# Who gets the eight PSUM banks in a two-layer hybrid decoder trunk: two for turned tiles, three for the input projection, the output projection in the scores' banks

## The chip, the cores and the metric

The kernel runs on one core of a Trainium2 chip. The metric is device time in microseconds (us) of the whole launch: inputs are in HBM at its start, the output is in HBM at its end. The work is done by TensorE (matrix multiplications and, through a multiplication with the identity, transposes), VectorE (DVE), ScalarE (ACT), GpSimd (POOL, here only a few memsets) and the DMA queues. Matmul results land in PSUM, which has eight banks; a bank holds one tile of 128 x 512 fp32 values. "Turned" below means transposed on TensorE.

## The reference

The sequence has S = 512 tokens of width D = 1024, the trunk has two layers, everything is fp32. Cut to what matters:

```python
for l in range(2):
    h = rms_norm(x, norm_mix_pre[l])
    q_da, k_da, v_da, q_r, k_r, v_r, g_r, u_pool = split(h @ w_in[l])     # 1024 -> 2560
    o_da   = diff_attention(q_da, k_da, v_da, ...)   # 4 heads: softmax(q1 k1) - lam * softmax(q2 k2), causal, times v
    o_ret  = retention(q_r, k_r, v_r, g_r, ...)      # 4 heads, chunks of 128: inside a chunk, and a state carried on
    o_pool = pool_mixer(u_pool, ...)                 # means over trailing windows 2/4/8/16, then 64x64 products
    mix = concat([o_da, o_ret, o_pool]) @ w_out[l]   # 1024 -> 1024
    x = x + rms_norm(mix, norm_mix_post[l])
    h = rms_norm(x, norm_mlp_pre[l])
    gate, val = split(causal_conv3(h @ w_up[l]))     # 1024 -> 5632
    x = x + rms_norm((gelu(gate) * val) @ w_down[l], norm_mlp_post[l])    # 2816 -> 1024
```

## The kernel before

**Tiles.** The tokens make four tiles of 128 (t or i, 0 to 3). Weights stay in no buffer for long: they stream through in units of 512 KB, read by SP's DMA queue into three raw buffers. ACT rounds each unit to the short format that TensorE multiplies fast (`wa`/`wb`, the high part, L275/L286), DVE takes what rounding left over (the low part, L276/L287). A product of full accuracy is three matmuls: high x high, high x low, low x high. The same holds for activations: `ht` is the normed input turned, high and low part; `qh`/`ql` the queries, `ks` the keys, `mixc` the concatenated head outputs.

**Order.** TensorE's order is written out: `mm` and `tr` (L321 to L325; all rows of the trace for TensorE carry L322 for a matmul and L325 for a transpose) chain each instruction to the one before. The main line of a layer is the input projection in five groups of 512 columns (`in_item`, group s = 0 queries, 1 keys, 2 values, 3 retention's keys and values, 4 gate and pooled input), the output projection, the up projection in 11 groups (`up_item`) and the down projection (`project` is both the output and the down projection). Between its matmuls stand small steps of the head groups, as tasks, each with a due time in the table PLACE; `serve` lets a task issue its next step when TensorE's count of columns has reached that time and what it names as needed has been issued. The order of ACT and DVE is set by a scheduler that sees which instruction waits for which.

**The tasks,** each of which opens a PSUM tile:
- `turned` in `qk_done` (L601): a query or key tile, scaled by ACT (L598), is turned into a `b` tile; `q_split` (ACT L616, DVE L619) or `k_split` (ACT L625, DVE L626) reads it out in two parts.
- `unit_a` (L676): scores of one head, map and token tile into an `s` tile; DVE masks, ACT takes the exponential (L689).
- `unit_b` (L698): the softmax weights turned into a `b` tile, which ACT copies out (L705).
- `unit_c` (L708): weights times values into the `o` tile.
- `unit_e` (L737): a token tile's head outputs turned into a `b` tile, read out by ACT (L734) and DVE (L735).
- `row_line` (L648), `ret_1` to `ret_4` (L749 to L812), `pool_mm` (L831): further users of `b`. `ret_3` also opens the update of the state, `bu`, in an `s` tile, which DVE reads at L785.
- Of the input projection's `m` tiles, ACT reads queries and keys at L598 and values at L629, DVE the retention values at L637 to L639, and the last group at L664 and, for the pooled input, L669. `finish_token` (L437) reads the tiles of the output and down projections.

**Banks.** `bank(tag)` takes a tile from a pool that deals by turns among the banks of its tag:

```python
BUFS = {"m": 4, "s": 2, "b": 1, "o": 1}
def bank(tag, shape=(P, 512)):
    return pp.tile(list(shape), F32, tag=tag, name=nm("ps_" + tag), bufs=BUFS[tag])
```

So the projections have four banks, the scores two, everything turned one, the values one. The first matmul into a tile waits until all readers of the tile that stood in its bank before are done. The output projection takes two banks for each token tile: `m`, `m` for tiles 0 and 1, `s`, `s` for 2, and `b`, `o` for 3.

Of the kernel before, what the change touches and what calls it, by code (L numbers as in the profile page):

```python
# [11 lines left out]
F32 = mybir.dt.float32  # L12
# [8 lines left out]
P = 128  # L21
# [4 lines left out]
KC = D // P  # L26
DFF = 2816
NFF = DFF // P
# [109 lines left out]
def tile_trunk(ctx: ExitStack, tc: tile.TileContext, x, xt, win, wout, wup, wdown, gpost, par, lam, const, out):  # L138
# [14 lines left out]
    def nm(s):  # L153
        uid[0] += 1
        return f"{s}_{uid[0]}"

    BUFS = {"m": 4, "s": 2, "b": 1, "o": 1}

    def bank(tag, shape=(P, 512)):
        return pp.tile(list(shape), F32, tag=tag, name=nm("ps_" + tag), bufs=BUFS[tag])  # L160

    ROLES = {"any": list(range(8)), "p0": [0, 1, 2], "p1": [3, 4], "aT": [5, 6], "on": [7], "g": [2]}
    turn = {r: 0 for r in ROLES}
# [383 lines left out]
    q_order = (0, 1, 2, 3)  # L547

    for l in range(DEPTH):
# [222 lines left out]
        def ret_3(c):  # L772
            ind, kq, kz = ret.pop(c)
            b = bank("b")
            if c > 0:
                mm(b[:, 0:256], lhsT=kq[:, P:2 * P], rhs=st_bd[0], start=True, stop=False, skip_group_check=True)
            for h in range(4):
                mm(b[:, 64 * h:64 * h + 64], lhsT=ind[:, h * P:(h + 1) * P], rhs=vr[:, c, 64 * h:64 * h + 64],
                          start=(c == 0), stop=True, skip_group_check=True)
            if c < NT - 1:  # L780
                bu = bank("s")
                mm(bu[:, 0:256], lhsT=kz, rhs=vr[:, c, :], start=True, stop=True)
                ns = one.tile([P, 256], F32, tag="state", name=nm("state"), bufs=2)
                bm = C("bm").unsqueeze(2).to_broadcast([P, 4, 64])
                ve.tensor_tensor(out=ns.rearrange("p (h d) -> p h d", h=4), in0=bu[:, 0:256].rearrange("p (h d) -> p h d", h=4), in1=bm, op=ALU.mult)  # L785
                if c > 0:
                    ve.scalar_tensor_tensor(ns, st_bd[0], C("cd"), ns, op0=ALU.mult, op1=ALU.add)
                st_bd[0] = ns
            oc = rtok[c // 2][:, c % 2, :]
            ov = oc.rearrange("p (h d) -> p h d", h=4)  # L790
            se.copy(oc, b[:, 0:256])
            sq = t2("p1", 256)
            se.activation(sq, oc, AF.Square)
            ss = small(4)
            ve.tensor_reduce(ss, sq.rearrange("p (h d) -> p h d", h=4), axis=AX.X, op=ALU.add)
            r = head_rsqrt(ss, 4, 64)
            ve.tensor_tensor(out=ov, in0=ov, in1=r.unsqueeze(2).to_broadcast([P, 4, 64]), op=ALU.mult)
            on_of[c] = oc
# [95 lines left out]
        banks = {}  # L894

        def in_item(s, j, t, rel, *cs):
            if (s, t) not in banks:
                banks[s, t] = bank("m")
            u = u0 + 4 * s + j
            (item_feat if s == 4 else item_tok)(banks[s, t], j, t, u, *cs)  # L900
            if rel:
                release(u)
            if j == 3:
                with ahead(300):
                    dones[s](banks.pop((s, t)), t)

        for s in range(5):
            od = q_order if s == 0 else range(NT)
            plan = [(j, t) for ts in (od[0:2], od[2:4]) for j in range(4) for t in ts]
            if s == 0 and l:  # L910
                plan = [(j, t) for t in od for j in range(4)]
            elif s == 0:
                plan = [(0, t, (c,)) for c in range(2) for t in od] + [(1, t) for t in od] + [(j, t) for t in od for j in (2, 3)]
            for n, (j, t, *cs) in enumerate(plan):
                if t not in row and j == 2:
                    row_factors(t)
                main(lambda: in_item(s, j, t, all(x[0] != j for x in plan[n + 1:]), *cs), u0 + 4 * s + j,
                     *[(l, "xT", x) for x in ((t,) if s < 4 else range(NT))])
            if s == 1:
                for gen in (turns(), values(), outputs(), scores()):  # L920
                    task(gen)
            if s == 3:
                for c in range(NT):
                    task(retention(c))
# [3 lines left out]
        def project(kn, lhs, plan, tags, u0, gain, needs, then, hook=None):  # L928
            ys = {}
            gp = None  # L930

            def item(k, t, cols, rel):
                if t not in ys:
                    ys[t] = [bank(tg) for tg in tags[t]]
                lh, ll = lhs(k, t)
                wh, wl = halves[u0 + k]
                for a, w, first in ((lh, wh, True), (lh, wl, False), (ll, wh, False)):
                    for h in cols:
                        mm(ys[t][h], lhsT=a, rhs=w[:, h * 512:(h + 1) * 512],
                           start=(k == 0 and first), stop=(k == kn - 1 and w is wh and a is ll))  # L940
                    serve(512 * len(cols))
                if rel:
                    release(u0 + k)

            for n, (k, t, *cols) in enumerate(plan):
                if hook is not None:
                    hook(k)
                if k == kn - 1 and gp is None:
                    gp = gain()
                main(lambda: item(k, t, cols or (0, 1), all(x[0] != k for x in plan[n + 1:])), u0 + k, *needs(k, t))  # L950
                if k == kn - 1 and cols != [0]:
                    with ahead(300):
                        finish_token(t, ys[t], gp)
                        then(t, tags[t])
# [29 lines left out]
        def mixed(k, t):  # L984
            if k == 0 and t == 2:
                return (l, "e", NT - 1), (l, "r4", NT - 1), (l, "p", 0), (l, "p", 1)
            return ((l, "e", t) if k < 4 else (l, "r4", t) if k < 6 else (l, "p", k - 6),)
        project(KC, mix_lhs, plan, {0: ("m", "m"), 1: ("m", "m"), 2: ("s", "s"), 3: ("b", "o")},
                unit[0], lambda: load_gain(2 * l), mixed, next_mlp)
        state["space"] = []  # L990
        unit[0] += KC
# [41 lines left out]
        bks = {}  # L1033

        def up_item(g, j, ft, a, b):
            tags = ["m"] * 4 if g % 2 == 0 else ["s", "s", "b", "o"]
            fresh = (g, ft) not in bks
            if fresh:
                bks[g, ft] = bank(tags[ft])
            u = u0 + 4 * g + j  # L1040
            k = dict(skip_group_check=True) if g == 1 and ft < 2 else {}
            item_feat(bks[g, ft], j, ft, u, a, b, fresh or not k, **k)
            if b == S and ft == 3:
                release(u)
            if b == S and j == 3:
                up_done(bks.pop((g, ft)), g, ft)
# [38 lines left out]
        def act_lhs(k, t):  # L1085
# [5 lines left out]
        plan += [(k, t) for k in range(2, NFF - 7) for t in range(NT)]  # L1091
        plan += [(k, t) for t in q_order[:3] for k in range(NFF - 7, NFF)]
        plan += [(k, q_order[3], h) for h in range(2) for k in range(NFF - 7, NFF)]
        project(NFF, act_lhs, plan, {0: ("s", "s"), 1: ("b", "o"), 2: ("m", "m"), 3: ("m", "m")},
                unit[0], lambda: gain2, lambda k, t: (), store if l == DEPTH - 1 else next_mixer, hook)
        state["space"] = []
        unit[0] += NFF
# [42 lines left out]
```

## Time and profile before

| | us |
|---|---|
| runs | 1155.54, 1155.96, 1156.54 |
| median | 1155.96 |
| the profiled execution | 1154.14 |
| its span in the trace | 1152.3 |

The span goes from the first to the last instruction that the profiler shows; the execution's own time has what lies around it as well. Clocks in the trace count from the span's start. In rows of the profile, engines are PE (TensorE's matmuls), PEld (its weight loads), DVE, ACT, POOL and SP; `ps_b<-cst,t` is a tile written from tiles read, with the numbers of tiles left out; an instruction's row gives its start, its duration, how many were grouped (x4), and in brackets the idle time of the engine just ahead of it, with the instruction that ended last among those that it waited for. In the first layer the input projection with the tasks runs to about 160 us, the output projection opens there, and the second layer's mixer begins about 610 us.

### The profile page before, as it was taken

To read this page: it belongs to the slowest core of one execution; us is meant where nothing else is said; L and a number is where in the kernel's file an instruction comes from. 1 tells how busy PE (TensorE), PEld (TensorE's weight loads), DVE (VectorE), ACT (ScalarE), POOL (GpSimd) and SP (SyncE) were. 2 spreads that over 40 slices of the span, in tenths; PEclk is the share of its full clock that TensorE was granted. 3 is DMA by queue.
4 is the path that set the end of the run, shared out by engine and by line. 5 is a ranking of instruction groups with operands and counts; after the bars stand their busy time and mean duration, and the time that the engine had idled before them with its cause. 6 is when DMAs were issued, how large, how long until landed. Compare 5 with 4: busy or idle time off the path is not lost.

```text
span 1152.3 us, 14840 instructions
## 1 busy us (share of the span) xinstructions
PE 1135.6 (99%) x5474; PEld 943.6 (82%) x5474; DVE 740.6 (64%) x1669; ACT 547.5 (48%) x1049; POOL 12.0 (1%) x20
## 2 busy tenths in 40 slices
PE   9999999999999999999999999999999999999997
PEld 6788778988888888888888887789888888888885
DVE  6988696877556457423777896877855655663224
ACT  6966553565444345313466754444744434452211
POOL 1000000000000000000000000000000000000000
PEclk9999999999999999999999999999999999999999
DMA  8411131332222232224033111303323232223311
GB/s 325 147 55 56 55 113 40 111 128 91 100 102 85 101 106 95 98 95 143 4 103 114 59 61 45 111 20 127 121 100 108 78 107 104 98 80 104 105 42 55
DMA packets 31320, 109.22 MB, mean 95 GB/s; under 512 B 3728, under 2 KB 4240, under 8 KB 31248
## 3 DMA queue, kind: packets, MB, share of 16 engines
q1 hardware_dynamic: 29808, 105.11, 26.4%
q10 hardware_dynamic: 1440, 3.17, 0.8%
q8 instruction: 43, 0.70, 0.2%
q14 instruction: 29, 0.24, 0.1%
HBM read 106.16 MB, written 2.10 MB: 94 GB/s over the span
## 4 chain that ended last, share of the span: by engine, by line
PE 93%; DVE 2%; ACT 2%; DMA 1%; issue 0%; SPq 0%; DVEq 0%; ACTq 0%
PE ps_m L322 52%; PE ps_s L322 18%; PE ps_b L322 10%; PE ps_o L322 10%; PE ps_b L325 2%; DMA raw<-in_win 1%; ACT t L689 1%; ACT wa L286 1%; PE ps_m L325 0%; DMA raw<-in_wout 0%; DVE ks L626 0%; DVE wb L287 0%; PE ps_s L325 0%; DVE wa L287 0%; DVE sm L687 0%
## 5 line engine op out<-in xcount | busy, mean ns | idle before, releaser
L322 PE MATMUL ps_m<-ht,wb 128*128 128x512 f32 (+1 forms) x768 | 197.9, 366 | 0.0
L322 PE MATMUL ps_m<-ht,wa 128*128 128x512 f32 (+1 forms) x768 | 197.2, 365 | 0.0
L287 DVE SCALAR_TENSOR_TENSOR wa<-raw,par,wa 128x512 fp32r<-128x512 f32 x128 | 95.7, 748 | 145.8 <-ACT wa L286 145.6
L286 ACT ACTIVATE wa<-raw,par 128x512 fp32r<-128x512 f32 x128 | 92.2, 721 | 188.0 <-PE ps_m L322 93.6
L322 PEld LDWEIGHTS ps_m<-ht,wa 128*128 128x128 f32 x768 | 135.2, 189 | 22.9 <-issue 1.0
L322 PEld LDWEIGHTS ps_m<-ht,wb 128*128 128x128 f32 x768 | 135.2, 189 | 22.7 <-issue 1.0
L322 PE MATMUL ps_m<-wa,ht 128*128 128x512 f32 x512 | 147.9, 396 | 0.4 <-ACT ht L504 0.3
L322 PE MATMUL ps_m<-wb,ht 128*128 128x512 f32 x448 | 129.3, 394 | 0.0
L322 PEld LDWEIGHTS ps_m<-wa,ht 128*128 128x128 f32 x512 | 93.4, 189 | 19.2 <-ACT ht L504 1.0
L276 DVE TENSOR_TENSOR wb<-raw,wa 128x1024 fp32r<-128x1024 f32 x38 | 46.6, 1225 | 81.9 <-ACT wa L275 81.9
L287 DVE SCALAR_TENSOR_TENSOR wb<-raw,par,wb 128x512 fp32r<-128x512 f32 x128 | 95.7, 747 | 4.5 <-ACT wb L286 4.4
L322 PEld LDWEIGHTS ps_m<-wb,ht 128*128 128x128 f32 x448 | 82.5, 188 | 16.3
L286 ACT ACTIVATE wb<-raw,par 128x512 fp32r<-128x512 f32 x128 | 91.9, 719 | 3.9 <-PE ps_m L322 3.2
L275 ACT CAST wa<-raw 128x1024 fp32r<-128x1024 f32 x38 | 39.9, 1051 | 86.7 <-PE ps_m L322 78.7
L322 PE MATMUL ps_s<-ht,wb 128*128 128x512 f32 (+1 forms) x264 | 69.1, 370 | 0.0
L322 PE MATMUL ps_s<-ht,wa 128*128 128x512 f32 (+1 forms) x264 | 69.0, 370 | 0.0
L322 PE MATMUL ps_m<-wa,c 128*128 128x512 f32 x224 | 65.7, 399 | 1.3 <-DVE pooled L669 1.3
L322 PEld LDWEIGHTS ps_s<-ht,wa 128*128 128x128 f32 x264 | 47.5, 188 | 8.6
L322 PEld LDWEIGHTS ps_s<-ht,wb 128*128 128x128 f32 x264 | 47.4, 188 | 8.4
L322 PEld LDWEIGHTS ps_m<-wa,c 128*128 128x128 f32 x224 | 41.6, 188 | 11.4 <-DVE pooled L669 2.2
L689 ACT ACTIVATE t<-ps_s,sm 128x128 f32<-128x128 f32 (+3 forms) x64 | 33.5, 527 | 21.5 <-DVE sm L687 18.8
L1010 ACT ACTIVATE t<-ps_m,par 128x512 f32<-128x512 f32 x48 | 36.5, 774 | 12.0 <-PE ps_m L322 12.0
(314 smaller groups left out, 1884.6 us busy)
## 6 DMA issues: line engine op xcount, KB each, us to landing
raw<-in_wup SPq DMA_DIRECT2D x88, 512.0 KB, 3.4
raw<-in_wdown SPq DMA_DIRECT2D x44, 512.0 KB, 3.4
raw<-in_win SPq DMA_DIRECT2D x39, 512.0 KB, 3.6
raw<-in_wout SPq DMA_DIRECT2D x16, 512.0 KB, 3.5
xs<-in_x SPq DMA_DIRECT2D x4, 512.0 KB, 9.6
gain<-in_gpost ACTq DMA_DIRECT2D x4, 512.0 KB, 5.0
t<-in_xt SPq DMA_DIRECT2D x3, 512.0 KB, 6.1
out<-xs SPq DMA_DIRECT2D x4, 256.0 KB, 2.0
```

Source lines behind the costliest of these rows:

```text
L275: se.copy(h, r)
L276: ve.tensor_tensor(out=lo, in0=r, in1=h.bitcast(F32), op=ALU.subtract)
L286: se.activation(a, x, AF.Copy, scale=sc)
L287: ve.scalar_tensor_tensor(b, x, sc, a.bitcast(F32), op0=ALU.mult, op1=ALU.subtract)
L322: in_order(te.matmul(out, lhsT=lhsT, rhs=rhs, **k))
L325: in_order(te.transpose(out, in_, ident))
L689: se.activation(p[:, 0:n], sb[:, 0:n], AF.Exp, bias=top, accum_out=sums[:, m:m + 1])
L1010: se.activation(acc, ps, AF.Identity, bias=conv[:, f, 3:4], scale=conv[:, f, 2:3])
```

## The change

It replaces the pool's dealing by a table of banks. What is turned (`b`) gets two, numbers 6 and 3, the input projection (`m`) three instead of four, 0 to 2; the scores keep two (4, 5), the values one (7). The output projection, the up and the down projection no longer name roles but banks, written out for each token tile or group (OUT_BANKS, DOWN_BANKS, UP_BANKS). The input projection's first group of four tiles opens in four banks that are named too: 0, 1, 2 and 4 in the first layer, 4, 5, 1 and 2 in the second. The state's update `bu` moves from `s` to `b`. In whole:

```diff
--- before.py
+++ after.py
@@ -154,10 +154,22 @@
         uid[0] += 1
         return f"{s}_{uid[0]}"
 
-    BUFS = {"m": 4, "s": 2, "b": 1, "o": 1}
-
-    def bank(tag, shape=(P, 512)):
-        return pp.tile(list(shape), F32, tag=tag, name=nm("ps_" + tag), bufs=BUFS[tag])
+
+
+    BANKS = {"m": (0, 1, 2), "s": (4, 5), "b": (6, 3), "o": (7,)}
+    took = dict.fromkeys(BANKS, 0)
+
+    def bank(role, shape=(P, 512)):
+        k = role
+        if role in BANKS:
+            k = BANKS[role][took[role] % len(BANKS[role])]
+            took[role] += 1
+        return pp.tile(list(shape), F32, tag=f"bank{k}", name=nm(f"ps_{role}"), bufs=1)
+
+
+    OUT_BANKS = {0: (4, 5), 1: (1, 2), 2: (0, 7), 3: (6, 3)}
+    DOWN_BANKS = {0: (0, 7), 1: (6, 3), 2: (4, 5), 3: (1, 2)}
+    UP_BANKS = ((4, 5, 1, 2), (0, 7, 6, 3))
 
     ROLES = {"any": list(range(8)), "p0": [0, 1, 2], "p1": [3, 4], "aT": [5, 6], "on": [7], "g": [2]}
     turn = {r: 0 for r in ROLES}
@@ -778,7 +790,7 @@
                 mm(b[:, 64 * h:64 * h + 64], lhsT=ind[:, h * P:(h + 1) * P], rhs=vr[:, c, 64 * h:64 * h + 64],
                           start=(c == 0), stop=True, skip_group_check=True)
             if c < NT - 1:
-                bu = bank("s")
+                bu = bank("b")
                 mm(bu[:, 0:256], lhsT=kz, rhs=vr[:, c, :], start=True, stop=True)
                 ns = one.tile([P, 256], F32, tag="state", name=nm("state"), bufs=2)
                 bm = C("bm").unsqueeze(2).to_broadcast([P, 4, 64])
@@ -895,7 +907,7 @@
 
         def in_item(s, j, t, rel, *cs):
             if (s, t) not in banks:
-                banks[s, t] = bank("m")
+                banks[s, t] = bank("m" if s else ((4, 5, 1, 2) if l else (0, 1, 2, 4))[q_order.index(t)])
             u = u0 + 4 * s + j
             (item_feat if s == 4 else item_tok)(banks[s, t], j, t, u, *cs)
             if rel:
@@ -904,6 +916,7 @@
                 with ahead(300):
                     dones[s](banks.pop((s, t)), t)
 
+        took["m"] = 0
         for s in range(5):
             od = q_order if s == 0 else range(NT)
             plan = [(j, t) for ts in (od[0:2], od[2:4]) for j in range(4) for t in ts]
@@ -985,7 +998,7 @@
             if k == 0 and t == 2:
                 return (l, "e", NT - 1), (l, "r4", NT - 1), (l, "p", 0), (l, "p", 1)
             return ((l, "e", t) if k < 4 else (l, "r4", t) if k < 6 else (l, "p", k - 6),)
-        project(KC, mix_lhs, plan, {0: ("m", "m"), 1: ("m", "m"), 2: ("s", "s"), 3: ("b", "o")},
+        project(KC, mix_lhs, plan, OUT_BANKS,
                 unit[0], lambda: load_gain(2 * l), mixed, next_mlp)
         state["space"] = []
         unit[0] += KC
@@ -1033,7 +1046,7 @@
         bks = {}
 
         def up_item(g, j, ft, a, b):
-            tags = ["m"] * 4 if g % 2 == 0 else ["s", "s", "b", "o"]
+            tags = UP_BANKS[g % 2]
             fresh = (g, ft) not in bks
             if fresh:
                 bks[g, ft] = bank(tags[ft])
@@ -1091,7 +1104,7 @@
         plan += [(k, t) for k in range(2, NFF - 7) for t in range(NT)]
         plan += [(k, t) for t in q_order[:3] for k in range(NFF - 7, NFF)]
         plan += [(k, q_order[3], h) for h in range(2) for k in range(NFF - 7, NFF)]
-        project(NFF, act_lhs, plan, {0: ("s", "s"), 1: ("b", "o"), 2: ("m", "m"), 3: ("m", "m")},
+        project(NFF, act_lhs, plan, DOWN_BANKS,
                 unit[0], lambda: gain2, lambda k, t: (), store if l == DEPTH - 1 else next_mixer, hook)
         state["space"] = []
         unit[0] += NFF
```

All line numbers behind the table are 12 higher in the changed kernel (13 from the loop over the input projection's groups on): L322 becomes L334, L325 L337.

No instruction is added or removed; TensorE, SP and POOL issue in the same order as before. What differs is which semaphores TensorE's instructions wait for and, on ACT and DVE, the places of a few instructions. In the order below, a name carries its role and two running numbers, `x3` are three instructions alike, and the brackets name the engines whose semaphores an instruction waits for.

TensorE in the first layer's mixer, where the weights of one head (`t2_270`) and of the next (`t2_290`) are turned, with input projection between and scores (`ps_s`) behind; in the trace of before the second turning is at 123.25. Before:

```order
L322 MATMUL ps_m_282_1305<-wa_198_970,ht_82 128x512 x3
L325 MATMUL ps_b_314_1449<-cst_80,t2_270_1256 128x128 [waits DVE_49]
L325 MATMUL ps_b_314_1449<-cst_80,t2_270_1256 128x128 x3
L322 MATMUL ps_m_282_1305<-wb_199_971,ht_82 128x512 x3
L322 MATMUL ps_m_318_1469<-ht_82,wa_215_1031 128x512 x3
L325 MATMUL ps_b_319_1473<-cst_80,t2_290_1346 128x128 [waits Activation_49]
L325 MATMUL ps_b_319_1473<-cst_80,t2_290_1346 128x128 x3
```

Now:

```order
L334 MATMUL ps_m_282_1305<-wa_198_970,ht_82 128x512 x3
L337 MATMUL ps_b_314_1449<-cst_80,t2_270_1256 128x128 [waits PE_49]
L337 MATMUL ps_b_314_1449<-cst_80,t2_270_1256 128x128 x3
L334 MATMUL ps_m_282_1305<-wb_199_971,ht_82 128x512 x3
L334 MATMUL ps_m_318_1469<-ht_82,wa_215_1031 128x512 x3
L337 MATMUL ps_b_319_1473<-cst_80,t2_290_1346 128x128 [waits DVE_49]
L337 MATMUL ps_b_319_1473<-cst_80,t2_290_1346 128x128 x3
```

The order is the same. The second turning waited for ACT, which copies the first turning's tile `ps_b_314` out of the one bank; now it opens in the other bank, and its wait is for DVE.

TensorE where the output projection opens, behind a retention step's product (`ps_b_387`, `ret_2`), in the trace of before from 160 us on. `wa_311`/`wb_312` are its first weights, `c1_46` the head outputs. Before:

```order
L322 MATMUL ps_b_387_1810<-t4_381_1770 128x512 [waits DVE_49,Activation_49,Pool_49]
L322 MATMUL ps_m_391_1831<-wa_311_1440,c1_46_221 128x512
L322 MATMUL ps_m_392_1832<-wa_311_1440,c1_46_221 128x512
L322 MATMUL ps_m_391_1831<-wb_312_1441,c1_46_221 128x512
L322 MATMUL ps_m_392_1832<-wb_312_1441,c1_46_221 128x512
L322 MATMUL ps_m_391_1831<-wa_311_1440,c1_46_221 128x512
L322 MATMUL ps_m_392_1832<-wa_311_1440,c1_46_221 128x512
L322 MATMUL ps_m_394_1843<-wa_311_1440,c1_46_221 128x512 [waits DVE_49]
L322 MATMUL ps_m_395_1844<-wa_311_1440,c1_46_221 128x512 [waits DVE_49]
```

Now (tiles of banks dealt by number are named by it: `ps_4` is bank 4):

```order
L334 MATMUL ps_b_387_1810<-t4_381_1770 128x512 [waits DVE_49,PE_49,Pool_49]
L334 MATMUL ps_4_391_1831<-wa_311_1440,c1_46_221 128x512
L334 MATMUL ps_5_392_1832<-wa_311_1440,c1_46_221 128x512
L334 MATMUL ps_4_391_1831<-wb_312_1441,c1_46_221 128x512
L334 MATMUL ps_5_392_1832<-wb_312_1441,c1_46_221 128x512
L334 MATMUL ps_4_391_1831<-wa_311_1440,c1_46_221 128x512
L334 MATMUL ps_5_392_1832<-wa_311_1440,c1_46_221 128x512
L334 MATMUL ps_1_394_1843<-wa_311_1440,c1_46_221 128x512
L334 MATMUL ps_2_395_1844<-wa_311_1440,c1_46_221 128x512 [waits DVE_49]
```

Again the order is the same. The first token tile's two halves open in banks 4 and 5 instead of two `m` banks; the second's (`391` and `392` are the first's, `394` and `395` the second's) in 1 and 2, and of its two waits for DVE one is left.

ACT in the first layer, where the first key tile (`ps_b_108`) and the second (`ps_b_112`) have been turned and are rounded into `ks`, among the rounding of weights (`wa`, `wb`). Before:

```order
L286 ACTIVATE wa_109_603<-raw_90_441,par_4_87 128x512
L286 ACTIVATE wb_110_604<-raw_90_441,par_4_87 128x512
L625 CAST ks_41_216<-ps_b_108_591 64x4x128
L286 ACTIVATE wa_115_639<-raw_94_456,par_4_87 128x512
L625 CAST ks_41_216<-ps_b_108_591 64x4x128
L286 ACTIVATE wb_116_640<-raw_94_456,par_4_87 128x512
```

Now:

```order
L637 CAST ks_41_216<-ps_b_108_591 64x4x128
L298 ACTIVATE wa_109_603<-raw_90_441,par_4_87 128x512
L298 ACTIVATE wb_110_604<-raw_90_441,par_4_87 128x512
L637 CAST ks_41_216<-ps_b_108_591 64x4x128
L298 ACTIVATE wa_115_639<-raw_94_456,par_4_87 128x512
L298 ACTIVATE wb_116_640<-raw_94_456,par_4_87 128x512
```

The first rounding of the key tile stood behind the weights `wa_109` and `wb_110` and now stands ahead of them; the second has kept its place.

## The prediction

> **What bounds the kernel now.** I read the page first, then the list of who waits for whom on TensorE, then the matmuls in order of time around the longest waits, then what ACT and DVE do there.
>
> ```profile
> span 1152.3 us, 14840 instructions
> PE 1135.6 (99%) x5474; PEld 943.6 (82%) x5474; DVE 740.6 (64%) x1669; ACT 547.5 (48%) x1049; POOL 12.0 (1%) x20
> PEclk9999999999999999999999999999999999999999
> ```
>
> TensorE is the bound: it is marked busy for 99% of the span, at full clock throughout. Its order of work is written out in the program, so only two things can shorten the kernel: less work on TensorE (the change removes none) or shorter waits between its instructions. The next row is from the chain of work, and the one after it from the groups by form.
>
> ```profile
> 259.07 21.76 PE ps_m L322 x96
> ```
> ```profile
> L322 PE MATMUL ps_b<-ht,wb 128*128 128x512 f32 x120 | 33.7, 389 | 0.0
> ```
>
> In the long steady stretch 96 matmuls take 21.76 us, so one starts every 227 ns, while a row lasts 389 ns: neighbours overlap by 162 ns. A wait therefore costs 0.16 us more than the idle time printed for it, which begins only when the modelled end of the last matmul is past. With this I read TensorE's waits (in total, times, longest):
>
> ```profile
> PE ps_b L325 <- ACT t L705: 2.9, 4, 1.2
> PE ps_b L325 <- DVE ql L619: 1.5, 1, 1.5
> PE ps_m L322 <- DVE pooled L669: 1.3, 2, 0.7
> PE ps_b L325 <- DVE ks L626: 0.6, 2, 0.4
> PE ps_b L325 <- DVE sm L385: 0.3, 2, 0.2
> PE ps_b L322 <- DVE t L808: 0.2, 1, 0.2
> ```
>
> Five of the six rows open a tile in `b`, the one bank in which everything is turned; the third opens the output projection in an `m` bank. Together 6.8 us of idle time in 12 waits, so 6.8 + 12 x 0.16 = 8.7 us. This is the pot. Gaps below the view's threshold may add some tenths.
>
> **Are these waits for the bank, or for data?** The matmuls of the first layer that waited, each with the idle time ahead of it:
>
> ```profile
> 49.16 0.63 PE L325 MATMUL ps_b<-cst,t 128*128 128x128 f32 x4 [1.47 <-DVE ql L619]
> 53.59 0.63 PE L325 MATMUL ps_b<-cst,t 128*128 128x128 f32 x4 [0.38 <-DVE ks L626]
> 71.92 0.33 PE L325 MATMUL ps_b<-cst,t 128*128 128x128 f32 x1 [0.25 <-ACT t L705]
> 123.25 0.66 PE L325 MATMUL ps_b<-cst,t 128*128 128x128 f32 x4 [1.22 <-ACT t L705]
> 153.65 0.41 PE L325 MATMUL ps_b<-cst,rtok 128*128 128x128 f32 x2 [0.16 <-DVE sm L385]
> 160.62 0.50 PE L322 MATMUL ps_m<-wa,c 128*128 128x512 f32 x1 [0.66 <-DVE pooled L669]
> ```
>
> And the readers of the tile that stood in the same bank before:
>
> ```profile
> 48.17 0.84 DVE L619 SCALAR_TENSOR_TENSOR ql<-ps_b,c 64x256 fp32r<-64x256 f32 x3
> 122.61 0.58 ACT L705 COPY t<-ps_b 128x512 f32<-128x512 f32 x1
> 152.82 0.68 DVE L735 TENSOR_TENSOR c<-ps_b,c 128x512 fp32r<-128x512 f32 x1
> 159.88 0.69 DVE L669 TENSOR_TENSOR pooled<-ps_m,rt 128x512 f32<-128x512 f32 x1
> ```
>
> They end at 49.01, 123.19, 153.50 and 160.57, and TensorE goes on 0.15, 0.06, 0.15 and 0.05 us later. (At 153.65 the view names L385, a small DVE step just before; the bank's reader is L735.) None of the four reads or makes what the waiting matmul takes in: L619 splits a turned query while a key is to be turned, L705 copies another head's weights. So it is the bank. In the second layer:
>
> ```profile
> 637.13 0.30 PE L325 MATMUL ps_b<-cst,t 128*128 128x128 f32 x1 [0.23 <-DVE ks L626]
> 641.50 0.33 PE L325 MATMUL ps_b<-cst,t 128*128 128x128 f32 x1 [0.25 <-ACT t L705]
> 692.82 0.66 PE L325 MATMUL ps_b<-cst,t 128*128 128x128 f32 x4 [1.22 <-ACT t L705]
> 723.27 0.41 PE L325 MATMUL ps_b<-cst,rtok 128*128 128x128 f32 x2 [0.17 <-DVE sm L385]
> 730.26 0.50 PE L322 MATMUL ps_m<-wa,c 128*128 128x512 f32 x1 [0.66 <-DVE pooled L669]
> 733.47 0.70 PE L322 MATMUL ps_b<-state,t 128*128 128x256 f32 x2 [0.17 <-DVE t L808]
> ```
>
> **The change part by part.** No instruction is added or taken away on any engine; TensorE, SP and POOL keep their order, so every weight load is issued behind the same work as before. ACT and DVE move a few reads of `b` tiles some places earlier. What changes is which older tile must be read out before a matmul may open a new one.
>
> *Two banks for what is turned (6 and 3, by turns).* A tile waits for the tile before last, not for the last. At 49.16 that is the tile two back, read long before. Gross gain by the rows, each idle time plus 0.16: 1.63 and 0.54 at 49.16 and 53.59, 0.41 at 71.92, 0.39 and 0.41 at 637.13 and 641.50, together 3.38 in the first half of the two mixers; 1.38 each at 123.25 and 692.82, 2.76; 0.32, 0.33 and 0.33 at 153.65, 723.27 and 733.47, 0.98.
>
> *The output projection opens in the scores' banks (4 and 5, then 1 and 2).* The scores are done when it opens, and banks 1 and 2 hold the third and second last tiles of the input projection; the last one, which L669 reads to 160.57, is in bank 0. The waits at 160.62 and 730.26 go: 2 x 0.82 = 1.64.
>
> How much of it is kept? TensorE's advance is worth something only if what it meets next is ready. The stretches (busy us of PE, PEld, DVE, ACT):
>
> ```profile
> 40.00:50.00 10.00, 8.51 (x42) 6.60 (x41) 8.89 (x26) 9.07 (x17) 0.00 (x0) 1.00 0.48 157
> 57.60:126.00 68.40, 66.75 (x360) 55.95 (x359) 60.89 (x195) 43.13 (x128) 1.07 (x2) 1.00 0.20 70
> 120.00:126.00 6.00, 4.78 (x29) 3.90 (x28) 6.00 (x17) 3.95 (x9) 0.00 (x0) 1.00 0.63 214
> 126.00:140.00 14.00, 14.00 (x79) 11.60 (x78) 6.09 (x17) 4.87 (x12) 0.00 (x0) 1.00 0.01 2
> 160.00:165.00 5.00, 4.38 (x23) 3.45 (x24) 4.99 (x12) 2.29 (x5) 0.00 (x0) 1.00 0.49 125
> ```
>
> DVE is full from 120 to 126 and from 160 to 165, but behind each it has room: 7.9 us idle in 126 to 140. It ends no later than before, TensorE only goes on while it works. So I keep 2.76 + 0.98 + 1.64 = 5.4 us whole. The first half is another matter. The matmuls below are what TensorE meets next, the other rows what they need:
>
> ```profile
> 54.92 0.68 DVE L626 TENSOR_TENSOR ks<-ps_b,ks 64x512 fp32r<-64x512 f32 x1
> 56.13 0.40 PE L322 MATMUL ps_s<-ks,c 128*128 128x256 f32 x2
> 40.60 1.27 ACT L598 ACTIVATE t<-ps_m,row 128x512 f32<-128x512 f32 x2 [0.56 <-DVE row L382]
> 42.10 0.85 PE L322 MATMUL ps_m<-wa,ht 128*128 128x512 f32 x3
> 124.26 0.48 DVE L639 SCALAR_TENSOR_TENSOR vr<-ps_m,row,sm 128x256 f32<-128x256 f32 x1
> 126.61 0.95 PE L322 MATMUL ps_m<-ht,wa 128*128 128x512 f32 x3
> ```
>
> The first scores at 56.13 need the split of the second key tile, ready at 55.60 + 0.15: a margin of 0.38. TensorE would come 2.17 earlier, so the split must come 1.8 earlier or TensorE waits there instead. It can start earlier, since TensorE turns that key earlier; but DVE and ACT are busy for 8.89 and 9.07 of the 10 us before. I let the split gain 1.4 and take off 0.4. Behind it, scores (two banks of their own, unchanged) wait for ACT's exponential, which waits for DVE; DVE has 7.5 us idle in the 68.4 from 57.6 on. For the smaller gains there (0.17 to 0.41 each) I take off half, and another 0.3 for the scores: the first half keeps 3.38 - 0.4 - 0.6 - 0.3 = 2.1. Its ends are 0 (all of it comes back as waits for DVE before 117) and 3.38; 2.1 lies nearer the upper one since DVE's idle 7.5 us is twice what it has to make up.
>
> *Three banks for the input projection, and the state's update moved from `s` to `b`.* I cost these at nothing. What hides the lost bank: the tile at 42.10 now opens in the bank that ACT's second L598 read until 41.87, 0.23 earlier (0.06 needed), and nothing moves ahead of 42.10. The one at 126.61 opens in the bank that L639 read until 124.74, so from 124.89: 1.72 to spare, against 1.38 gained just before; an advance from the first half shifts DVE too. If that cover goes, TensorE waits for ACT or DVE there and all matmuls behind it with it. The update makes a retention step take both `b` banks, so the next step is as tied as before, no more. A loss of up to 0.5 us is my lower end, a gain is excluded.
>
> *The banks of the up and down projections* go by the same pairs of token tiles as before: the gate's first groups open where the first two tokens' output stood. Nothing, with ends of 0.3 on both sides.
>
> Sum: 5.4 + 2.1 = 7.5 us. The profiled execution took 1154.14 us, 1.84 more than its span, and the median of the runs is 1155.96, 0.16% above it. So I expect a span near 1144.8, a profiled time of 1146.6 and a median of 1155.96 - 7.5 = **1148.5 us**.
>
> **The rivals.**
>
> *The first half is given back.* For it: DVE and ACT nearly full from 40 to 50, and a margin of 0.38 at 56.13. Against: DVE's idle time later. 5.4 us remain: 1150.6.
>
> *The readers are the bound, not the bank.* A second bank lets TensorE run ahead, to wait for the same DVE and ACT a few matmuls on. For it: DVE 6.00 of 6.00 around 123.25. Then 2.76 and 3.38 both come back, and 0.98 + 1.64 = 2.6 remain: 1153.3. Against: after 123.25 the next matmul that needs the copy of 122.61 is the one with the values, behind 4 matmuls of scores, and the copy ends 123.19, about when TensorE, 1.38 earlier, gets there.
> [...]
>
> *Slower: three banks are too few.* The third bank of the input projection is still unread when a tile wants it, at 126.61 above all, where DVE is full. Sixteen tiles a layer rotate through the three, 32 in all; to lose the 7.5 and 2.3 more takes 9.8 / 32 = 0.31 us at each, so a reader about 2 us later than now at 126.61 and 0.5 at 42.10. Nothing in the change makes readers later. From 1158.3 on.
>
> *It doesn't do what it says.* If neighbours among the turned tiles fell into one bank, the waits would stay: 1155.96. They are dealt by turns, so only tiles two apart meet.
>
> **How the numbers follow.** The forecast (6.3 us and more gained) has 0.62, the first half given back 0.22, the readers as the bound 0.08, three banks too few 0.05, no effect 0.03. About 0.2%, 2.3 us, is what a measurement of this kernel can tell from no change. Faster: 0.62 + 0.22 + half of 0.08 = 0.88; same: 0.04 + 0.03 = 0.07; slower 0.05. The range runs from a gain of 9.6 (the pot, with gaps under the threshold and the ends above) to one of 4.2 (5.4 less the losses of 0.5 and 0.3 and a little for the runs): 1146.4 to 1151.8, with some 0.82.
>
> **What the profile will show.** If right: no TensorE wait of L325 on ACT L705 or DVE L619 over 0.3 us, the waits on L669 gone, and TensorE's matmuls at 123.25, 160.62 and 692.82 follow their neighbours without a gap. A new, short wait of scores for L626 near 54 shows the 0.4. Wrong: a wait of `ps_m` on L598 or L639 (the third bank), or of `ps_o` on L705 and `ps_s` on L689 as long as those that went (the readers).

## The result, and the profile after

The changed kernel takes 1147.72 us (median of 6 runs, 1146.99 to 1147.92), the kernel before 1155.46 (6 runs, the three above among them, 1154.62 to 1156.54): 7.7 us less, a ratio of 0.9931 with an interval of 0.9920 to 0.9941. Forecast were 1148.5 and a gain of 7.5. One execution among the experiments below ran at a mean granted clock of 0.752 and took 1418.71 us; it is left out of its kernel's median.

The first lines of the page after:

```profile
span 1146.0 us, 14829 instructions
PE 1134.1 (99%) x5474; PEld 944.3 (82%) x5474; DVE 739.4 (65%) x1669; ACT 546.9 (48%) x1049; POOL 12.0 (1%) x20
```

The instructions on the five engines are as many as before (the total, 11 lower, also counts semaphore instructions); the span is 6.3 us shorter. TensorE's waits after (what waited, for whom, total, times, longest), lines 12 higher than before:

```profile
PE ps_o L334 <- DVE t L505: 1.2, 1, 1.2
PE ps L334 <- ACT ht L516: 1.1, 1, 1.1
PE ps_s L334 <- DVE ks L638: 0.4, 1, 0.4
PE ps_b L334 <- DVE t L820: 0.4, 2, 0.2
PE ps_s L334 <- ACT t L701: 0.4, 2, 0.2
PE ps L334 <- DVE ht L517: 0.2, 1, 0.2
```

The six rows of the prediction's list are gone: the waits for L717 (before L705), L631 (L619) and L681 (L669) don't appear. The row for L820 (before L808) looks like the old one but belongs to other matmuls: before, a product with the state waited at 733.47 (`ps_b<-state,t`); now the state's update waits, once in each layer (`ps_b<-vr,t`, shown below). New are also scores that wait for the key's split (L638) and for the exponential (L701). The rows for L505, L516 and L517 belong to the start of the launch.

At the places of the prediction's rows (49.16, 123.25, 160.62, 692.82, 723.27, 730.26), the timeline after:

```profile
48.47 0.60 PE L337 MATMUL ps_b<-cst,t 128*128 128x128 f32 x4
121.34 0.60 PE L337 MATMUL ps_b<-cst,t 128*128 128x128 f32 x4
156.83 1.09 PE L334 MATMUL ps<-wa,c 128*128 128x512 f32 x4
687.94 0.60 PE L337 MATMUL ps_b<-cst,t 128*128 128x128 f32 x4
717.99 0.39 PE L337 MATMUL ps_b<-cst,rtok 128*128 128x128 f32 x2
723.42 1.09 PE L334 MATMUL ps<-wa,c 128*128 128x512 f32 x4
```

None has idle time ahead of it: at 156.83 four matmuls of the output projection stand in one group, where before the fourth waited 0.66.

Since TensorE issues the same matmuls in the same order in both, the k-th of one trace is the k-th of the other, and the difference of their starts shows where time was gained and lost. Below, a jump is the change of that difference from one matmul to the next, which needs no correction for overlap.

| stretch (us, clock of before) | what it holds | forecast | traces |
|---|---|---|---|
| 0 to 44.5 | the start | 0 | +1.13 |
| 44.5 to 80 | first half, layer 0 | | -1.68 |
| 632 to 650 | first half, layer 1 | | -0.41 |
| both first halves | | -2.1 | -2.09 |
| 100 to 170 | second half, layer 0 | | -2.55 |
| 650 to 740 | second half, layer 1 | | -2.76 |
| both second halves | | -5.4 | -5.31 |

The start is not the change's work: TensorE waits there for ACT's rounding of the input, 0.26 us in the profiled execution before and 1.11 in this one, where ACT itself had waited 1.89 us for weights from a DMA (L298 at 17.26). In the other profiled executions below that wait is 0.45 to 1.59 us long. From 44.5 on the difference is 7.45 us, close to that of the medians.

### The profile page after: what moved, and what is told of

Read it like the earlier page. It is cut to its first block, busy times and chain, and to the rows that moved or that the text cites. A ratio compares the mean times of both kernels' runs of the same rounds, so it can differ in the third digit from the quotient of the medians.

```text
span 1146.0 us, 14829 instructions
## 1 busy us (share of the span) xinstructions
PE 1134.1 (99%) x5474; PEld 944.3 (82%) x5474; DVE 739.4 (65%) x1669; ACT 546.9 (48%) x1049; POOL 12.0 (1%) x20
## 4 chain that ended last, share of the span: by engine, by line
PE 89%; DVE 4%; ACT 4%; DMA 2%; issue 1%; SPq 0%; DVEq 0%; ACTq 0%
PE ps L334 72%; PE ps_m L334 10%; PE ps_b L334 2%; PE ps_o L334 2%; PE ps_b L337 2%; PE ps_s L334 1%; PE ps L337 1%; DMA rt<-in_lam 1%; DMA raw<-in_wout 1%; DVE ks L638 1%; ACT wa L298 1%; DMA raw<-in_win 1%; ACT t L610 0%; ACT t L701 0%; ACT c L628 0%
## 5 line engine op out<-in xcount | busy, mean ns | idle before, releaser
L334 PE MATMUL ps<-ht,wb 128*128 128x512 f32 (+1 forms) x1176 | 305.0, 368 | 0.0
L334 PE MATMUL ps<-ht,wa 128*128 128x512 f32 (+1 forms) x1176 | 304.8, 367 | 0.0
L334 PEld LDWEIGHTS ps<-ht,wa 128*128 128x128 f32 x1176 | 210.3, 188 | 36.5
L334 PEld LDWEIGHTS ps<-ht,wb 128*128 128x128 f32 x1176 | 210.1, 188 | 36.5
L298 ACT ACTIVATE wa<-raw,par 128x512 fp32r<-128x512 f32 x128 | 92.2, 721 | 185.1 <-PE ps L334 173.4
L334 PE MATMUL ps<-wa,c 128*128 128x512 f32 x448 | 126.3, 394 | 0.0
L334 PE MATMUL ps<-wa,ht 128*128 128x512 f32 x352 | 98.2, 392 | 1.3 <-ACT ht L516 1.1
L334 PEld LDWEIGHTS ps<-wa,c 128*128 128x128 f32 x448 | 83.6, 188 | 18.0 <-issue 1.0
L298 ACT ACTIVATE wb<-raw,par 128x512 fp32r<-128x512 f32 x128 | 91.9, 720 | 4.3 <-PE ps L334 3.1
L334 PE MATMUL ps_m<-wa,ht 128*128 128x512 f32 x288 | 83.6, 398 | 0.0
L334 PE MATMUL ps_m<-wb,ht 128*128 128x512 f32 x288 | 83.3, 397 | 0.0
L1023 ACT ACTIVATE t<-ps,par 128x512 f32<-128x512 f32 x88 | 67.5, 774 | 24.9 <-PE ps L334 24.9
L334 PEld LDWEIGHTS ps<-wa,ht 128*128 128x128 f32 x352 | 65.7, 188 | 16.1 <-ACT ht L516 1.9
L334 PE MATMUL ps<-wb,c 128*128 128x512 f32 x224 | 71.8, 397 | 0.0
L334 PE MATMUL ps<-wb,ht 128*128 128x512 f32 x224 | 66.3, 389 | 0.0
L334 PEld LDWEIGHTS ps_m<-wb,ht 128*128 128x128 f32 x288 | 52.5, 188 | 10.1
```

The lines of the kernel that those rows point to most:

```text
L298: se.activation(a, x, AF.Copy, scale=sc)
L334: in_order(te.matmul(out, lhsT=lhsT, rhs=rhs, **k))
L1023: se.activation(acc, ps, AF.Identity, bias=conv[:, f, 3:4], scale=conv[:, f, 2:3])
```

## The experiments

The runs of one kernel lie 1 us and more apart, so differences of half a microsecond are read from the traces by the jumps; where the text gives a time, it is the median.

**The output projection's opening alone.**

```diff
-    BANKS = {"m": (0, 1, 2), "s": (4, 5), "b": (6, 3), "o": (7,)}
+    BANKS = {"m": (0, 1, 2, 3), "s": (4, 5), "b": (6,), "o": (7,)}
...
-                bu = bank("b")
+                bu = bank("s" if c < 2 else 7)
```

> Only the output projection's opening is changed: four banks (0 to 3) for the input projection and one (6) for what is turned, as before; the state's update stays in the scores' banks for the first two chunks and goes to bank 7 for the third, since the scores' banks are taken there. Theory (each part is worth its own waits): the two waits for L669 go, 2 x 0.82 = 1.6 us, all waits at the one bank stay, so 1153.8 where the kernel before has 1155.5; in the trace the matmuls of the wait for L705 at 123.25 and of the wait for L619 at 49.16 wait as long as before. Rival (the wait at the opening comes back as a wait for the one bank a little later): 1155.5. Rival (the opening carries most of the gain, the turned tiles' waits were only shown, not paid): 1148 to 1150.

It took 1155.25, ratio 0.9999 (0.9990 to 1.0008). From its list of waits, and from its timeline:

```profile
PE ps_b L337 <- ACT t L717: 3.0, 4, 1.2
PE ps_b L334 <- DVE t L820: 2.1, 2, 1.3
PE ps_b L337 <- DVE ql L631: 1.5, 1, 1.5
```
```profile
161.82 1.09 PE L334 MATMUL ps<-wa,c 128*128 128x512 f32 x4
166.31 0.70 PE L334 MATMUL ps_b<-state,t 128*128 128x256 f32 x2 [0.88 <-DVE t L820]
736.20 0.70 PE L334 MATMUL ps_b<-state,t 128*128 128x256 f32 x2 [1.27 <-DVE t L820]
```

The waits at the opening are gone (161.82), by -0.92 and -0.92 (a jump of -0.8 and one of -0.1 right behind it); 3.5 to 4.5 us later the retention's next tile waits in the one bank for L820, by jumps of +0.89 and +1.10. The waits of the other turnings stay as they were (2.9 and 1.5 us before, 3.0 and 1.5 here). The first rival holds: alone, this part is worth nothing, since the one bank takes back what it gains. What it is worth beside a second bank for turned tiles comes next.

**Everything but the opening.** The input projection's banks are dealt from another start, so that its last tile lies where the output projection's second token tile opens.

```diff
-banks[s, t] = bank("m" if s else ((4, 5, 1, 2) if l else (0, 1, 2, 4))[q_order.index(t)])
+banks[s, t] = bank("m" if s else ((4, 5, 0, 1) if l else (2, 0, 1, 4))[q_order.index(t)])
...
-        took["m"] = 0
+        took["m"] = 2
```

> Two banks for what is turned and three for the input projection as in the changed kernel, but the input projection's banks are dealt from another start, so that its last tile, which the pooling's L681 reads, lies in bank 2, where the output projection's second token tile opens: the wait that the change removed there is put back. Theory: 0.82 us more than the changed kernel in each layer, 1.6 in all, so 1149.3 where the changed kernel has 1147.7; everything ahead of the opening as in the changed kernel. Rival (the opening carries most of the gain): 1153 to 1155. Rival (the start of the dealing matters for the third bank, whose margin is near nothing at one tile): up to 1 us more or less, seen as waits of the input projection's tiles for L610.

It took 1148.11 (ratio 0.9936, 0.9922 to 0.9949); the medians lie only 0.4 us apart, but by the traces it needs 0.62 and 0.59 us more than the changed kernel, from 44.5 to 170 and from 170 to 740.

```profile
158.15 0.50 PE L334 MATMUL ps<-wa,c 128*128 128x512 f32 x1 [0.79 <-DVE pooled L681]
161.45 1.49 PE L334 MATMUL ps_b<-vr,t 128*128 128x64 f32 x10
```

The wait for L681 is back as expected, but the wait for L820 of the changed kernel (below) is not there: TensorE, about 1 us later (jumps of 0.95 and 0.10), finds that tile read, and the update runs in one group with the products ahead of it (161.45). So the opening is worth 1.2 us and not 1.64, as it hands some of its gain on to that wait. Everything else carries the rest, 6.2 of 7.45, above all the two banks for what is turned. The last rival shows too, ahead of 44.5 and so outside these sums: with the other start of the dealing two matmuls of the input projection come later than in the changed kernel, by jumps of 0.25 at 30.59 and 0.12 at 42.80.

**The state's update in a bank of its own.**

```diff
-                bu = bank("b")
+                bu = bank("b" if c < 2 else 0)
```

> The changed kernel, but the state's update of the third chunk opens in bank 0, which is free there, instead of the next bank of what is turned. Theory (moving the update cost 0.37 in each layer, a wait for the reader of the tile two back, L820): that wait goes, 0.7 us less than the changed kernel, so 1147.0, and TensorE's matmul of the update follows without a gap. Rival (the retention's chain of readers sets the pace there, and the next step waits in its place): as the changed kernel, 1147.7, with a new wait within 3 us behind.

First the changed kernel's rows, with the reader that TensorE waits for in the first layer, then this kernel's:

```profile
161.45 0.41 DVE L820 TENSOR_TENSOR t<-ps_b,sg 128x256 f32<-128x256 f32 x1
161.92 0.48 PE L334 MATMUL ps_b<-vr,t 128*128 128x256 f32 x1 [0.21 <-DVE t L820]
728.51 0.48 PE L334 MATMUL ps_b<-vr,t 128*128 128x256 f32 x1 [0.21 <-DVE t L820]
```
```profile
161.94 0.65 PE L334 MATMUL ps<-vr,t 128*128 128x256 f32 x2
728.25 0.65 PE L334 MATMUL ps<-vr,t 128*128 128x256 f32 x2
```

Both waits go, by jumps of -0.38 each, and nothing behind them is lost again. 1147.27 (ratio 0.9929, 0.9916 to 0.9941): 0.45 less than the changed kernel, of the right sign, though the runs of the two overlap (1146.72 to 1147.81 here). By the traces it is 0.76 us better than the changed kernel.

**The first scores put off.**

```diff
-        [[152, 202], [208, 214], [221, 225], [191, 214]],
+        [[196, 202], [208, 214], [221, 225], [191, 214]],
```

> The changed kernel, but the first score of each layer is due 4 columns of 512 later than the start of its task (152 becomes 196), so that three matmuls of the input projection stand ahead of it. Theory (the 0.6 us given back at 55.5 in the first layer is the key's split being late, not TensorE): the wait for L638 there falls by the 0.69 us of these three matmuls to nothing, 0.5 to 0.6 less, 1147.2; the second layer has no wait there and stays. Rival (DVE and ACT are behind by as much for whatever comes next): the wait comes back at the next scores, which wait for L701, and the time stays at 1147.7.

1147.77 (0.9934, 0.9921 to 0.9946). The changed kernel's scores, then this kernel's and its next turning:

```profile
55.48 0.50 PE L334 MATMUL ps_s<-ks,c 128*128 128x256 f32 x2 [0.45 <-DVE ks L638]
```
```profile
55.28 0.47 PE L334 MATMUL ps_s<-ks,c 128*128 128x256 f32 x2
57.60 0.63 PE L337 MATMUL ps_b<-cst,t 128*128 128x128 f32 x4 [0.47 <-DVE t L595]
```

The jump of +0.61 at 55.48 is gone, one of +0.63 at 57.60 is new: the third key tile isn't rotated yet (L595). The rival holds in kind, the time is given back, but at a turning and for L595, not at the scores and for L701 as it had it. Why the key is late is next: is it DVE's load, or ACT's order?

**Less load on DVE.**

```diff
-                ve.scalar_tensor_tensor(b, x, sc, a.bitcast(F32), op0=ALU.mult, op1=ALU.subtract)
+                if 10 <= j < 14:
+                    ge.tensor_scalar(x, x, sc, None, op0=ALU.mult)
+                    ge.tensor_tensor(out=b, in0=x, in1=a.bitcast(F32), op=ALU.subtract)
+                else:
+                    ve.scalar_tensor_tensor(b, x, sc, a.bitcast(F32), op0=ALU.mult, op1=ALU.subtract)
```

> The changed kernel, but the remainders of four weight units of the first layer (those that DVE takes from 46 to 60 us, L299, 8 instructions of 0.75 us) are taken by POOL, which is idle there, in two steps each. Theory (what is given back at 55.5, 0.6 us, is DVE having no time for the key's split): DVE's four remainders ahead of L638 at 54.74 fall away, 2.7 us, the split comes earlier by at least 0.6 and the wait for L638 goes; the waits of scores for L701 at 69 may shrink too; 0.5 to 0.9 less than the changed kernel, 1147.0, if POOL takes under 3 us for each 128x512 step. Rival (ACT's rounding of the key, L637, which stands behind two roundings of weights, comes last, not DVE): the wait stays at 0.4 or more idle. Rival (POOL is slow or slows DVE): weights late at about 66, slower than 1148.

1150.25 (0.9958, 0.9944 to 0.9972), slower than the changed kernel. POOL's two kinds of step, DVE and ACT around the split (lines 4 higher), and TensorE:

```profile
45.84 1.57 POOL L300 TENSOR_SCALAR raw<-raw,par 128x512 f32<-128x512 f32 x1 [41.30 <-ACT wa L298]
47.49 1.29 POOL L301 TENSOR_TENSOR wa<-raw,wa 128x512 fp32r<-128x512 f32 x1
54.03 0.79 DVE L596 TENSOR_TENSOR rt<-t,cst 128x128 f32<-128x128 f32 x1 [1.39 <-ACT t L614]
55.05 0.68 DVE L642 TENSOR_TENSOR ks<-ps_b,ks 64x512 fp32r<-64x512 f32 x1
53.90 0.57 ACT L641 CAST ks<-ps_b 64x512 fp32r<-64x512 f32 x1
55.70 0.72 ACT L298 ACTIVATE wa<-raw,par 128x512 fp32r<-128x512 f32 x1 [1.23 <-DMA raw<-in_win]
55.79 0.51 PE L338 MATMUL ps_s<-ks,c 128*128 128x256 f32 x2 [1.12 <-DVE ks L642]
69.30 0.50 PE L338 MATMUL ps_s<-ks,c 128*128 128x256 f32 x2 [1.01 <-ACT t L705]
```

Without these remainders DVE idles 1.39 us, waiting for ACT, and still the split is no earlier: ACT's rounding, which it needs, starts at 53.90 behind other work, as the first rival has it; on this the theory fell. The split then starts at 55.05, 0.6 us behind the rounding's end, since DVE's step at 54.03 took 0.79 us where another of the same line took 0.29: it ended 0.15 us behind a step of POOL's (the last section has the rows), as the second rival has it. The scores lose 2.8 us more than in the changed kernel up to 70 us. How much of this is DVE's longer steps beside POOL's, and how much the weight for which ACT waited 1.23 us (55.70; POOL needs 2.86 us for what DVE does in 0.75, and holds the weight's buffer longer), was not told apart.

**ACT's order.** With the state's update in bank 0, the second key tile's first rounding ahead of two roundings of weights:

```diff
+                w = se.activation(a, x, AF.Copy, scale=sc)
+                if j == 12:
+                    tc.add_manual_dep(w.ins, keys[2].ins.name, ORDER, reason="key ahead of weights")
...
-                se.copy(ks[r, :, m, sl], bv[r])
+                keys.append(se.copy(ks[r, :, m, sl], bv[r]))
```

> The kernel with the state's update in bank 0, and on ACT in the first layer the rounding of the second key tile (L637's first half) placed ahead of the two roundings of a weight unit (L298) that stand before it; a dependence of order alone, no work is added or left out, TensorE's order is the same. Theory (the 0.6 us given back at 55.5 is ACT's order: the rounding stands behind two of weights and one of the input projection, 52.19 to 54.14, though the key is turned at 52.8): the rounding starts at about 53 or behind L610 at 53.5, the split is ready 0.6 to 1.2 earlier and the wait for L638 goes, 0.6 less than that kernel, 1146.6, provided that the next turning, which waited for L595 when the scores were put off, gets its tile earlier too. Rival (the time is lost again at the next turning or at the scores' banks, waits for L595 or L701): 1147.2, the wait only moves.

ACT in the changed kernel, then ACT, TensorE and DVE in this one:

```profile
52.19 0.72 ACT L298 ACTIVATE wa<-raw,par 128x512 fp32r<-128x512 f32 x1
52.82 0.71 ACT L298 ACTIVATE wb<-raw,par 128x512 fp32r<-128x512 f32 x1
53.55 0.69 ACT L610 ACTIVATE t<-ps_m,row 128x512 f32<-128x512 f32 x1
54.14 0.57 ACT L637 CAST ks<-ps_b 64x512 fp32r<-64x512 f32 x1
```
```profile
52.81 0.57 ACT L640 CAST ks<-ps_b 64x512 fp32r<-64x512 f32 x1
54.53 0.40 PE L337 MATMUL ps_s<-ks,c 128*128 128x256 f32 x2
61.92 0.39 PE L337 MATMUL ps_s<-ks,c 128*128 128x256 f32 x1 [1.26 <-ACT t L704]
59.32 0.59 ACT L640 CAST ks<-ps_b 64x512 fp32r<-64x512 f32 x1 [0.91 <-DVE ks L641]
60.30 0.69 DVE L641 TENSOR_TENSOR ks<-ps_b,ks 64x512 fp32r<-64x512 f32 x1
61.03 0.29 DVE L702 TENSOR_REDUCE sm<-ps_s 128x1 f32<-128x128 f32 x1
61.41 0.37 ACT L704 ACTIVATE t<-ps_s,sm 128x128 f32<-128x128 f32 x1 [1.51 <-DVE sm L702]
```

The rounding starts at 52.81 instead of 54.14, 1.0 us earlier when the 0.33 are taken off that this execution's start was shorter, and the wait for the split is gone, by -0.72 (jumps of -0.61 and -0.11): that wait was ACT's order. But at 61.92 scores wait 1.26 us (a jump of +1.35) for an exponential that follows, on ACT and DVE, another key's split. 1146.98 (0.9927, 0.9913 to 0.9940), which is that of the kernel with the update in bank 0 within the scatter; by the traces 0.2 us worse to 80 us. So the rival holds, and what TensorE can't keep there isn't the fault of one instruction's place. From 44.5 to 80 us it keeps 1.68 in the changed kernel, 1.69 with the update in bank 0, 1.65 with the scores put off and 1.49 here.

**One tile of the input projection in a spare bank.**

```diff
-banks[s, t] = bank("m" if s else ((4, 5, 1, 2) if l else (0, 1, 2, 4))[q_order.index(t)])
+banks[s, t] = bank(5 if (l, s, t) == (0, 1, 3) else "m" if s else ((4, 5, 1, 2) if l else (1, 2, 0, 4))[q_order.index(t)])
...
-        took["m"] = 0
+        took["m"] = 0 if l else 1
...
-                bu = bank("b")
+                bu = bank("b" if c < 2 else 0)
```

> The changed kernel with the state's update of the third chunk in bank 0, and in the first layer the last key tile of the input projection in bank 5, a scores' bank that nobody uses yet, instead of the third bank; the dealing starts one bank later, so that the last tile lies in bank 0 as in the changed kernel. Theory: the matmul at 43.08, which opens in the third bank, no longer waits for L610, 0.2 us, and the update's 2 x 0.38 stay away: 1.0 us less than the changed kernel, 1146.7. Rival (at 43 TensorE's advance is lost again at the next turning, since ACT and DVE are full): only the update's 0.8 remain, 1146.9.

1147.37 (0.9934, 0.9921 to 0.9948). At 43.08 the changed kernel has jumps of 0.10 at two neighbouring matmuls against the kernel before: that is what the third bank costs. With the spare bank they are gone, and the wait for the split at 55.81 has grown by 0.33. The rival holds, though the loss comes at the split and not already at the next turning: the 0.2 us cost nothing, since what is gained there is lost again.

```profile
55.81 0.39 PE L334 MATMUL ps_s<-ks,c 128*128 128x256 f32 x1 [0.78 <-DVE ks L638]
```

**The second token tile's scores put off,** in two goes, the second for its trace.

```diff
-        [[240, 240], [250, 224], [262, 241], [270, 272]],
+        [[244, 244], [250, 224], [262, 241], [270, 272]],
```

> The changed kernel, but the first scores of the second token tile are due 4 columns later (240 becomes 244), behind three more matmuls of the input projection. They are what waits for L701 at 69.45 and 636.04, for the scores' banks: 0.32 and 0.39 with the overlap. Theory (two banks of scores hold TensorE up there, now that the turned tiles don't): both waits go, as does some of the wait of the values for L717 behind them: 0.7 less, 1147.0. Rival (the order's other waits take it): the values (ps_o) come earlier and wait for their copies by as much, 1147.7.

> The kernel with the second token tile's first scores due 4 columns later once more, for a trace at full clock. It took 1 us more than the changed kernel where 0.7 less was expected. Theory now: the scores put off make everything behind them late, since they are a chain through two banks (scores, maximum, exponential, weights), so new waits for L701 or L717 of 1 to 1.5 us stand behind 70 and 637. Rival: the time is lost elsewhere, at the values (ps_o) that now come earlier.

The first took 1148.73 (3 runs; 0.9945, 0.9929 to 0.9960), the second, one run, 1149.20. A miss: 1.0 and 1.5 us slower than the changed kernel where 0.7 faster was expected. The trace of the second:

```profile
74.95 0.84 PE L334 MATMUL ps_s<-ks,c 128*128 128x256 f32 x3 [0.59 <-ACT t L701]
642.25 0.84 PE L334 MATMUL ps_s<-ks,c 128*128 128x256 f32 x3 [0.59 <-ACT t L701]
```

The scores' waits at 69.45 and 636.04 went and came back longer at the next scores, 5 to 6 us on, with jumps of +0.75 and +0.74 and about 0.1 at each of the three matmuls behind: of the kind that the second theory expected, but shorter than its 1 to 1.5. This fits a chain through the two scores' banks, TensorE to DVE to ACT and back, in which a start put off moves all that follows; no run gave the scores a third bank.

## Why the prediction was right, and where not

*The pot.* Each wait was the bank's, and each idle time plus 0.16 was its price: the jumps are -1.63 at 49.16 (forecast 1.63), -0.53 at 53.59 (0.54), -1.39 at 123.25 and 692.82 (1.38 each), -0.31, -0.32 and -0.34 at 153.65, 723.27 and 733.47 (0.32, 0.33, 0.33), -0.82 at 160.62 and 730.26 (0.82). The correction for overlap matters: by the printed idle times alone the pot would be 6.8, less than what was gained. But more was gained, and more given back, than the rows show: all downward jumps of 0.03 and more in the table's four half stretches come to 11.0 us, the upward ones to 3.7.

*The first half.* Forecast 2.1 of 3.38 kept, found 2.09. That the two meet is luck: twice as much was given back as forecast, 2.6 us instead of 1.3, and gains that the forecast didn't list made up for it, 1.3 us, among them -0.30 at 72.61 and at 642.18, at products with the values, -0.17 at 44.99 and -0.19 at 633.05, at turnings. Taken off for the scores behind the second key was 0.4, and the jump was 0.61 with 0.11 behind it; the half taken off the smaller gains (0.6) and the 0.3 for the scores answer to +0.32 and +0.39 for the scores' banks (L701) and +0.25 twice for the values (L717), each with 0.1 behind it. The cause named was also incomplete: not only DVE but ACT's place for one rounding, and behind that waits of scores and turnings, which three other orders only moved. The forecast's argument from DVE's idle 7.5 us said little: with DVE relieved, the wait was longer, though DVE's longer step beside POOL's (0.79 us instead of 0.29) is part of that. In this half the rival of the readers is right in part: 1.3 of the 3.38 came back on balance.

*The second half.* Forecast 5.4, found 5.31, with one step wrong. The state's update, moved to the turned tiles' banks, was costed at nothing, since "the next step is as tied as before". It is the update itself that waits: it opens in the bank of the tile two back, which L820 reads until 161.86, late because DVE is full there (busy for 2.00 of the 2 us from 160 to 162). That is 0.38 in each layer, 0.76 us, beyond the 0.5 that the step allowed as its worst, and the experiment with bank 0 took back just that. The sum hides it, again by luck: small gains that the forecast's rows don't show come to about 1.0, such as 0.11 at the matmul behind each opening's wait and 0.15 at 163.66.

*The opening of the output projection,* 1.64, was priced as if it stood alone. Alone it is worth nothing, and with the rest 1.2. That its two waits went was right; that what TensorE meets next must be ready was argued for DVE's room in the large, not for the one tile that comes 4 us later.

*Three banks for the input projection.* Costed at nothing with a margin of 0.17 at 42.10: that margin was used up (0.2 us), but without that loss the 0.2 are lost at the first scores instead. At 126.61 there is no jump above 0.1.

*The rivals.* The whole first half given back: no, 1.68 and 0.41 were kept. The slower one, three banks too few: no wait of that kind above 0.1 a matmul. The 7.7 us were gained at a mean granted clock of 0.999 before and 0.998 after, in the profiled executions.

## What to carry to other kernels

Here a wait for a bank was worth its idle time plus the overlap of neighbouring matmuls (0.16 us), and it was kept where what TensorE met next was ready (in the second halves, 5.3 of 5.4 on balance); where the readers form a chain back to TensorE, part of it came back (2.1 of 3.4 were left). Two changes that met the same reader were not worth the sum of their prices: the opening gained 0 alone and 1.2 beside the second bank. Before a tile is moved to another pool of banks, look up who read the tile that will stand there last, and when: the one move costed at nothing hid a loss of 0.76 us.

## What the hardware showed beside

*A low clock behind a short wait.* In the profiled execution of the opening alone, TensorE waited 1.59 us at the start (columns: stretch, its length; busy us and instructions of PE, PEld, DVE, ACT, POOL; granted clock; DMA share and GB/s):

```profile
18.00:19.00 1.00, 0.04 (x1) 0.00 (x0) 0.56 (x1) 1.00 (x3) 0.00 (x0) 1.00 1.00 399
21.00:22.00 1.00, 1.00 (x4) 0.75 (x3) 0.06 (x1) 0.00 (x0) 0.00 (x0) 0.50 1.00 384
23.00:24.00 1.00, 1.00 (x4) 0.81 (x3) 0.31 (x2) 1.00 (x4) 0.00 (x0) 0.50 1.02 418
```

For some 3 us the granted clock was 0.50, and between 18.5 and 44.5 us the execution lost 1.56 us more than the kernel before; it took 1157.07 where its kernel's median is 1155.25. Behind waits there of 1.11 us in the changed kernel's trace and 1.3 in that with the update in bank 0 the clock was 1.00 from 17 to 25 us and from 17 to 22 us. In this one execution the clock had fallen 1.4 us behind the end of a wait of 1.6 us; that the wait was the cause is not shown.

*DVE's steps beside POOL's.* Two of DVE's L596 in the experiment with POOL (that at 54.03 is shown above), and POOL's steps on two tensors:

```profile
47.03 0.29 DVE L596 TENSOR_TENSOR rt<-t,cst 128x128 f32<-128x128 f32 x1 [1.37 <-ACT t L614]
53.38 1.29 POOL L301 TENSOR_TENSOR wa<-raw,wa 128x512 fp32r<-128x512 f32 x1
56.45 1.29 POOL L301 TENSOR_TENSOR wb<-raw,wb 128x512 fp32r<-128x512 f32 x1
57.03 0.86 DVE L596 TENSOR_TENSOR rt<-t,cst 128x128 f32<-128x128 f32 x1 [0.90 <-ACT t L614]
```

Beside POOL's step on one tensor (L300, 45.84 to 47.41) the first took 0.29 us, as in the changed kernel (L592, 0.29 at 55.46). The steps at 54.03 and 57.03 began while POOL worked on two tensors (L301, to 54.67 and 57.74), ended 0.15 us behind it and took 0.79 and 0.86 us, 0.50 and 0.57 more than the first; what ties the two engines together there is not shown. So an idle POOL was not free here for a step on two tensors beside DVE's L596.
